# Half a fill tile set twice into the hand-made TensorE order of each of the first six attention steps

## The chip, the cores and the metric

The kernel runs on one core of a Trainium2 chip. The metric is the device time of one execution in microseconds (us). TensorE does the matmuls; VectorE, ScalarE and GpSimd do the element work; SyncE issues most of the transfers. In the rows they are called PE (its weight loads PEld), DVE, ACT, POOL and SP.

## The reference, cut to what matters

One layer on 1024 tokens of width 1024, float32. `x @ w_in` is split into three branches: an attention with three kinds of keys (compressed, selected, window), a gated MLP and an mLSTM. Their results are gated, merged, projected and normalised. The change concerns the attention and a few of the projections:

```python
(a_q, a_kc, a_vc, a_ks, a_vs, a_kw, a_vw, a_g, a_z,
 b_u, b_v, b_z,
 c_q, c_k, c_v, c_if, c_o, c_z, m_g) = jnp.split(x @ w_in[i], split_at, axis=-1)
y_a = _nsa(a_q, a_kc, ..., cmp_wv2[i]) * jax.nn.silu(a_z)
y_b = _spatial_gating(b_u, b_v, ..., sg_b[i]) * jax.nn.silu(b_z)
```

`_nsa` works on two groups of four heads. For each block of 128 queries it makes a softmax over 63 compressed keys; these weights also rank the 16 key blocks of which 8 are selected. A softmax over the selected keys and one over a window of 256 keys follow, and the three results are added with gates. `_spatial_gating` starts with `gelu(b_u)`.

## The kernel before

A float32 operand of a large product is held as the sum of two rounded halves (`hi`, `lo`), and three matmuls take the place of one. All large projections are made that way. A projection tile of 128 outputs by 1024 tokens is done in two halves of 512 tokens; a half is 8 x 3 = 24 matmuls into one bank of PSUM (`proj_half`, L127, PSUM tag `pj`, two banks).

Most of the program is put in order by a scheduler. In the attention (`attend`) the order of TensorE's instructions is written out by hand: inside `tc.manual_schedule` they go out as the code issues them. Instructions from outside that block may still be placed between them by the scheduler. The other engines are ordered by the scheduler. Each engine executes its own list.

`attend(g)` first makes keys and queries (`prep_group`: KA/KB, QA/QB; 144 matmuls of L127). Then follow nine steps. In step s:

- `attn_max(g, s)`: for each of four heads scores against the window keys (`ps_w`, L487) and the selected keys (`ps_s`, L495), and on VectorE the row maxima (`rowmax`, L408 and L411). At its end the maxima are transposed (`ps_m`, L502), and VectorE writes them into QB (L503).
- `Back(g, s-1)`: scores again, transposed and exponentiated (`ps_st`, L529 and L530, L532), values (`ps_o`, L557, with four updates of `o` on VectorE for each kind of key, L564 to L568), and in `finish` two transposes of the result (`ps_ot`, L574), copied to `ya` (L577).
- `attn_cmp`: compressed scores for query block s+1 (`ps_c`, L425), softmax on VectorE and ScalarE (`pcm`, L427 to L436), from block 4 on the ranking `rk` (L440 to L457). At the end of the step the weights are transposed (`ps_t`, L461), and from block 4 on the ranking is transposed too (`ps_r`, L466) and written into QB (L467). The product with the compressed values (`ps_co`, L471) comes in the next step.

`ps_c`, `ps_t`, `ps_r`, `ps_co`, `ps_w`, `ps_s` and `ps_m` share the PSUM tag `m`, which has two banks. So each of them also waits for the reader of the last but one.

Fill tiles are projections that the attention doesn't need: `fill_bu` (gelu), `fill_bz` and `fill_az` (silu), each 2 x 24 matmuls, with a ScalarE operation and one to three VectorE operations on each half (for `bu` L170 to L173; for `bz` L179, L180 and L607). Their weights are loaded, rounded on ScalarE (L90) and subtracted on VectorE (L91) in `load_w`. In the kernel before they are called after `attend`, outside the hand-made order: three `bu` and three `bz` behind group 0, the rest behind group 1.

Of the kernel before, what the change touches and what calls it, by code (L numbers as in the profile page):

```python
# [2 lines left out]

# [1 line left out]

# [18 lines left out]
KT = 8  # L24
# [19 lines left out]
def hybrid_kernel(ctx, tc, xm, pT, wfm, wvg, wtm, cmpw1, cmpw2, cpos, vecs, sgwT, sgb,  # L44
# [4 lines left out]
    stop = dbg.get("stop")  # L49
# [19 lines left out]
    def pj():  # L69
        return pst("pj", 2)  # L70

    mm = nc.tensor.matmul
# [48 lines left out]
    def proj_half(po, w, half, hs, ls, K=KT, M=P):  # L121
        wh, wl = w
        n = 3 * K
        i = 0
        for k in range(K):
            for a, b in ((wh, hs), (wl, hs), (wh, ls)):
                mm(po[:M, :], lhsT=a[:, k, :], rhs=b(k, half), start=(i == 0), stop=(i == n - 1))  # L127
                i += 1

    def proj_tok(po, ws, tt, n, hs, ls):  # L130
# [34 lines left out]
    def gelu2(dst, src, n):  # L165

        sq = tp.tile([P, 512], F32, tag="ge_a", bufs=2, name="ge_a")[:, :n]
        if len(src.shape) == 3:
            sq = sq.rearrange("p (a b) -> p a b", a=src.shape[1])
        act(sq, src, AF.Square, scale=GK)  # L170
        stt(out=sq, in0=sq, scalar=1.0, in1=src, op0=OP.add, op1=OP.mult)
        act(sq, sq, AF.Tanh, scale=GC)
        stt(out=dst, in0=sq, scalar=1.0, in1=src, op0=OP.add, op1=OP.mult)  # L173
# [79 lines left out]
    wh = pc.tile([P, 8, 288], F32R, name="wh")  # L253
    wl = pc.tile([P, 8, 288], F32R, name="wl")
# [3 lines left out]
    for m in range(4):  # L258
        for r, half in ((0, 0), (0, 1), (1, 0), (1, 1)) if m == 0 else ((0, 0), (1, 0), (0, 1), (1, 1)):
            k = 2 * m + r  # L260
            for kv, w in enumerate((wk, wv)):
                for i, (a, b) in enumerate(((w[0], xh), (w[1], xh), (w[0], xl))):
                    mm(pkv[kv][half], lhsT=a[:, k, :], rhs=b(k, half), start=(k == 0 and i == 0),
                       stop=(k == KT - 1 and i == 2))
# [16 lines left out]
    for kv in range(2):  # L281
        st = stk[kv]
        for half in range(2):
            po = pkv[kv][half]
            a = half * 512
# [17 lines left out]
    for tt in range(NT):  # L303
        po = pst("o", 2, "ps_v")
# [8 lines left out]
    for kv in range(2):  # L313
        st = stk[kv]
        ph = pst("m", 2)
        for v in range(2):
            zb = yp.tile([P, T], F32, tag="y", bufs=YB, name="zb")
            z4 = zb[:, 0:1008].rearrange("p (j g n) -> p j g n", j=8, g=2)
            for j in range(8):
                i = 16 * v + 2 * j  # L320
                nc.any.tensor_scalar(out=z4[:, j], in0=st[:, :, i:i + 993:16], scalar1=pos[:, kv, 8 * v + j:8 * v + j + 1],
                                     scalar2=None, op0=OP.add)
            for j in range(8):
                mm(ph[:, 0:126], lhsT=w1[kv][v][:, j, :], rhs=zb[:, j * 126:j * 126 + 126],
                   start=(v + j == 0), stop=(v + j == 8))
# [9 lines left out]
        else:  # L335
            pvc = pst("m", 2)
            for g in range(G):
                mm(pvc[0:63, g * 64:g * 64 + 64], lhsT=ge[:, g * 63:g * 63 + 63], rhs=w2[:, 1, :],
                   start=True, stop=True)
# [241 lines left out]
    def fill_az(i):  # L581
        w = wf(FM["az"] + i)
        for half in range(2):
            po = pj()
            proj_half(po, w, half, xh, xl)
            y = ya[i][:, half * 512:half * 512 + 512]
            z = tp.tile([P, 512], F32, tag="ge_a", bufs=2, name="zz")
            act(z, po, AF.Tanh, scale=0.5)
            stt(out=z, in0=z, scalar=1.0, in1=po, op0=OP.add, op1=OP.mult)
            stt(out=y, in0=z, scalar=0.5, in1=y, op0=OP.mult, op1=OP.mult)  # L590

    def fill_bu(i):
        w = wf(FM["bu"] + i)
        for half in range(2):
            po = pj()
            proj_half(po, w, half, xh, xl)
            gelu2(yb[i][:, half * 512:half * 512 + 512], po, 512)

    def fill_bz(i):
        w = wf(FM["bz"] + i)  # L600
        for half in range(2):
            po = pj()
            proj_half(po, w, half, xh, xl)
            z = tp.tile([P, 512], F32, tag="ge_a", bufs=2, name="zz")
            silu2(z, po, 512, z)
            y = yb[i][:, half * 512:half * 512 + 512]
            vv.tensor_mul(y, y, z)  # L607

    def attend(g):
        with tc.manual_schedule(engines={mybir.EngineType.PE}):
            d = prep_group(g)
            cmp_ = attn_cmp(g, 0, d)
            next(cmp_)
            next(cmp_)
            for step in range(NT + 1):
                back = Back(g, step - 1, d) if step else None
                mxs = attn_max(g, step, d) if step < NT else iter(())
                nmx = (4 + HPG * (1 + step // 4)) if step < NT else 0  # L620
                last = back.n if back else 2
                done = 0
                for k in range(last + 1):
                    upto = nmx * (k + 1) // (last + 1)
                    mid = (done + upto + 1) // 2
                    for _ in range(done, mid):
                        next(mxs)
                    if back and k < back.n:
                        back.scores(k)
                    for _ in range(mid, upto):  # L630
                        next(mxs)
                    done = upto
                    if k == 0:
                        if step < NT:
                            next(cmp_)
                        cmp_ = attn_cmp(g, step + 1, d) if step + 1 < NT else iter(())
                        next(cmp_, None)
                    if back and k:
                        back.values(k - 1)
                if back:  # L640
                    back.finish()
                next(mxs, None)
                next(cmp_, None)
    attend(0)
    for i in range(3):
        fill_bu(i)
        fill_bz(i)
    attend(1)
    fill_bu(3)
    fill_bz(3)  # L650
    for i in range(4):
        fill_az(i)
    if "ya" in dbg:
        for i in range(4):
            nc.sync.dma_start(dbg["ya"][i], ya[i])
# [387 lines left out]
    for b in range(3):  # L1043
# [7 lines left out]
        for n in range(8):  # L1051
            if n % 2 == 0:
                wb = load_w(wbr[b, n // 2], 8, P)
            w = (wb[0][:, 4 * (n % 2):4 * (n % 2) + 4, :], wb[1][:, 4 * (n % 2):4 * (n % 2) + 4, :])
# [19 lines left out]
    for n in range(8):  # L1074
        w = load_w(wout[n], KT, P)
# [3 lines left out]
        for half in range(2):  # L1079
            s = slice(half * 512, half * 512 + 512)  # L1080
            po = pj()
# [52 lines left out]
    for tt in range(NT):  # L1134
# [5 lines left out]
        for c in range(npc):  # L1140
            s = slice(c * n, c * n + n)
            pe = pst("m" if tt == 1 else "o", 2, "ps_e")
            i = 0
# [147 lines left out]
```

## Time and profile before

| | |
|---|---|
| device time, median of 3 runs | 1373.07 us (1372.04 to 1374.55) |
| profiled execution, its device time | 1371.17 us |
| span from its first to its last instruction | 1369.1 us |
| mean granted TensorE clock in it | 0.993 of full |
| TensorE busy | 1337.7 us, 98% of the span |
| VectorE busy | 844.4 us, 62% |
| ScalarE busy | 526.1 us, 38% |
| GpSimd busy | 152.8 us, 11% |

All rows come from one profiled execution. Times in rows count from the start of its span. A matmul's duration in a row includes its way through the array, and the next one starts before it ends; so the rate of a run of matmuls is read from the distance of their starts. A bracket at the end of a row gives the idle time of the engine ahead of the row and what ended it. The granted clock is 1.00 at 2.4 GHz and 0.50 at 1.2 GHz.

### The profile page before, as it was taken

How to read it: one execution, taken by the hardware profiler on the slowest of the kernel's cores; microseconds unless marked ns; L12 is line 12 of the kernel's file. 1: busy time of each engine (PE TensorE's matmuls, PEld its weight loads, DVE VectorE, ACT ScalarE, POOL GpSimd, SP SyncE). 2: the span in 40 equal slices, each digit the busy share in tenths (PEclk: the TensorE clock that was granted, in tenths of full speed). 3: DMA queues.
4: the chain of work that ended last, by engine and by line, in shares of the span. 5: the costliest groups of instructions: out<-in, count | busy, mean ns of one | idle time of the engine just before them, and what ended most of it. 6: DMA issues, size and time to landing. Idle time of an engine off the chain costs nothing.

```text
span 1369.1 us, 18928 instructions
## 1 busy us (share of the span) xinstructions
PE 1337.7 (98%) x7135; PEld 1130.5 (83%) x7135; DVE 844.4 (62%) x1991; ACT 526.1 (38%) x1059; POOL 152.8 (11%) x173
## 2 busy tenths in 40 slices
PE   8998999998999999999999999999999999999997
PEld 6986888886888899988888888888878887888786
DVE  6247777336777467647776678766544555334855
ACT  6354333344333343135455355553442212324211
POOL 0012211101120100001001000010000444000312
PEclk9999999999999999999999999999999999999999
DMA  9131001111002141333223332236346543114201
GB/s 316 32 71 50 24 28 28 38 48 43 9 24 69 41 155 54 132 108 124 82 73 108 108 110 79 81 120 212 108 169 208 194 152 108 47 62 126 105 32 47
DMA packets 48059, 127.46 MB, mean 93 GB/s; under 512 B 5208, under 2 KB 16344, under 8 KB 47968
## 3 DMA queue, kind: packets, MB, share of 16 engines
q1 hardware_dynamic: 47008, 123.11, 27.4%
q0 software_dynamic: 960, 3.15, 1.1%
q8 instruction: 56, 0.92, 0.3%
q14 instruction: 35, 0.29, 0.1%
HBM read 101.00 MB, written 25.23 MB: 92 GB/s over the span
## 4 chain that ended last, share of the span: by engine, by line
PE 90%; DVE 5%; ACT 2%; DMA 2%; issue 1%; SPq 0%; POOL 0%; DVEq 0%; ACTq 0%; POOLq 0%
PE ps_pj L127 19%; PE ps_a L837 14%; PE ps_b L127 9%; PE ps_b L837 8%; PE ps_o L557 7%; PE ps_g L1106 5%; PE ps_st L148 3%; PE ps_pj L148 3%; PE ps_c L837 3%; PE ps_st L529 2%; PE ps_st L530 2%; PE ps_v L136 2%; PE ps_e L1146 2%; PE ps_s L495 1%; PE ps_w L487 1%
## 5 line engine op out<-in xcount | busy, mean ns | idle before, releaser
L127 PE MATMUL ps_pj<-xh,whi 128*128 128x512 f32 x288 | 115.5, 401 | 2.3 <-DVE QA L401 2.3
L127 PE MATMUL ps_pj<-xh,wlo 128*128 128x512 f32 x288 | 115.2, 400 | 0.0
L127 PE MATMUL ps_pj<-xl,whi 128*128 128x512 f32 x288 | 114.6, 398 | 0.0
L557 PEld LDWEIGHTS ps_o<-V,pt 128*128 128x128 f32 x912 | 110.2, 191 | 3.4
L557 PE MATMUL ps_o<-V,pt 128*128 128x65 f32 x912 | 108.3, 271 | 0.0
L532 ACT ACTIVATE pt<-ps_st 128x512 f32<-128x512 f32 x114 | 62.8, 596 | 89.3 <-PE ps_st L530 88.6
L837 PE MATMUL ps_a<-op_lo,sh 128*128 128x512 f32 x240 | 94.1, 392 | 0.0
L837 PE MATMUL ps_a<-op_hi,sl 128*128 128x512 f32 x240 | 93.8, 391 | 0.0
L837 PE MATMUL ps_a<-op_hi,sh 128*128 128x512 f32 x240 | 93.8, 391 | 0.0
L824 DVE TENSOR_TENSOR sl<-ss,sh 128x512 fp32r<-128x512 f32 x80 | 54.8, 690 | 59.0 <-ACT sh L823 58.9
L90 ACT CAST whi<-wraw 128x1024 fp32r<-128x1024 f32 x46 | 48.3, 1049 | 94.8 <-PE ps_b L127 44.7
L127 PE MATMUL ps_b<-sp_hi,wlo 128*128 128x512 f32 x192 | 74.8, 390 | 1.3 <-DVE wlo L91 1.3
L127 PE MATMUL ps_b<-sp_lo,whi 128*128 128x512 f32 x192 | 74.7, 389 | 0.0
L91 DVE TENSOR_TENSOR wlo<-wraw,whi 128x1024 fp32r<-128x1024 f32 x46 | 62.3, 1353 | 19.7 <-ACT whi L90 15.5
L127 PE MATMUL ps_b<-sp_hi,whi 128*128 128x512 f32 x192 | 73.9, 389 | 0.0
L1065 POOL TENSOR_TENSOR M<-M,gt 128x512 f32<-128x512 f32 x32 | 43.8, 1378 | 199.1 <-DVE gt L1064 183.5
L127 PEld LDWEIGHTS ps_pj<-xh,whi 128*128 128x128 f32 x288 | 54.3, 188 | 13.7 <-PE ps_pj L127 3.9
L127 PEld LDWEIGHTS ps_pj<-xh,wlo 128*128 128x128 f32 x288 | 54.3, 188 | 10.0
L127 PEld LDWEIGHTS ps_pj<-xl,whi 128*128 128x128 f32 x288 | 54.3, 189 | 9.3
L823 ACT CAST sh<-mraw 128x512 fp32r<-128x512 f32 x60 | 37.4, 623 | 57.1 <-PE ps_a L837 30.8
L823 ACT CAST sh<-ss 128x512 fp32r<-128x512 f32 x80 | 49.6, 620 | 22.9 <-PE ps_b L837 22.1
L824 DVE TENSOR_TENSOR sl<-mraw,sh 128x512 fp32r<-128x512 f32 x60 | 43.6, 727 | 22.8 <-ACT sh L823 22.8
(369 smaller groups left out, 3534.2 us busy)
## 6 DMA issues: line engine op xcount, KB each, us to landing
mraw<-in_wfm_dram SPq DMA_DIRECT2D x40, 512.0 KB, 3.6
gsc<-gt SPq DMA_DIRECT2D x24, 512.0 KB, 2.6
gt<-gsc SPq DMA_DIRECT2D x24, 512.0 KB, 4.3
wraw<-in_wfm_dram SPq DMA_DIRECT2D x18, 512.0 KB, 3.5
xraw<-in_xm_dram SPq DMA_DIRECT2D x14, 512.0 KB, 5.5
yraw<-ysc SPq DMA_DIRECT2D x12, 512.0 KB, 3.4
wraw<-in_wbr_dram SPq DMA_DIRECT2D x12, 512.0 KB, 5.0
wraw<-in_wtm_dram SPq DMA_DIRECT2D x8, 512.0 KB, 4.0
```

Source lines behind the costliest of these rows:

```text
L90: nc.scalar.copy(hi[:, c], raw[:, c])
L91: vv.tensor_sub(lo[:, c], raw[:, c], hi[:, c])
L127: mm(po[:M, :], lhsT=a[:, k, :], rhs=b(k, half), start=(i == 0), stop=(i == n - 1))
L136: mm(po[:, :n], lhsT=tok(a, k, tt), rhs=b[:, k % 4, :], start=(i == 0), stop=(i == tot - 1))
L148: mm(po, lhsT=tok(a, 4 * i + k, tt), rhs=b[:, k, :], start=(i == 0 and tt % 2 == 0 and k == 0 and j == 0), stop=(i == 1 and k == 3 and j = ...
L532: act(pt.rearrange("p h q -> p (h q)"), sp, AF.Exp)
L557: mm(po[:, h * 65:h * 65 + 65], lhsT=pt[:, h, :], rhs=V[:, j, vi, :], start=(first and h == 0), stop=last, skip_group_check=True)
L823: nc.scalar.copy(hi, src)
L824: vv.tensor_sub(lo, src, hi)
L837: mm(bank, lhsT=l[a][:, k, :], rhs=r[b], start=first and k == 0 and i == 0, stop=k == K - 1 and i == 2, skip_group_check=True)
L1065: nc.gpsimd.tensor_add(M[n][:, s], M[n][:, s], t[:, s])
L1106: mm(po[:, 0:n], lhsT=a[k][:, ts_], rhs=b[k][:, s], start=(k == 0 and i == 0), stop=(k == KT - 1 and i == 2))
```

## The change

`fill_*` become generators. `proj_parts` does what `proj_half` did, and yields once in the middle; the fill functions pass that on and yield again behind each half with its epilogue. One `next(fills)` is therefore half a half tile: 12 matmuls. `attend` takes a generator and calls `next(fills)` twice in each of steps 0 to 5, inside the hand-made order: once behind the first row-maximum matmul of the step (ahead of the first scores), and once ahead of `back.finish()`. Twelve calls use up `bu(0)`, `bz(0)`, `bu(1)` in group 0 and `bu(3)`, `bz(3)`, `az(0)` in group 1. The other six fill tiles stay outside, called after `attend`, as all were.

```diff
+    def proj_parts(po, w, half, hs, ls):
+
+        wh, wl = w
+        i = 0
+        for k in range(KT):
+            if k == KT // 2:
+                yield
+            for a, b in ((wh, hs), (wl, hs), (wh, ls)):
+                mm(po, lhsT=a[:, k, :], rhs=b(k, half), start=(i == 0), stop=(i == 3 * KT - 1))
                 i += 1
...
     def fill_bu(i):
         w = wf(FM["bu"] + i)
         for half in range(2):
             po = pj()
-            proj_half(po, w, half, xh, xl)
+            yield from proj_parts(po, w, half, xh, xl)
             gelu2(yb[i][:, half * 512:half * 512 + 512], po, 512)
+            yield
...
-    def attend(g):
+    def attend(g, fills):
...
                     for _ in range(done, mid):
                         next(mxs)
+                    if k == 0 and step < 6:
+                        next(fills)
                     if back and k < back.n:
                         back.scores(k)
...
                     if back and k:
                         back.values(k - 1)
+                if step < 6:
+                    next(fills)
                 if back:
                     back.finish()
                 next(mxs, None)
                 next(cmp_, None)
-    attend(0)
-    for i in range(3):
-        fill_bu(i)
-        fill_bz(i)
-    attend(1)
-    fill_bu(3)
-    fill_bz(3)
-    for i in range(4):
-        fill_az(i)
+    fl = chain(fill_bu(0), fill_bz(0), fill_bu(1))
+    attend(0, fl)
+    for _ in chain(fl, fill_bz(1), fill_bu(2), fill_bz(2)):
+        pass
+    fl = chain(fill_bu(3), fill_bz(3), fill_az(0))
+    attend(1, fl)
+    for _ in chain(fl, fill_az(1), fill_az(2), fill_az(3)):
+        pass
```

How the lists of the engines move is shown at two places. The fills carry the line L127 before and L139 after; the other lines move down by 12 or a little more (L425 becomes L437, L461 L473, L487 L499, L502 L514, L503 L515, L568 L580, L574 L586). The text keeps the numbers of before. A line of "..." stands for more rows of the same run of fills.

TensorE at the head of group 0, from the compressed scores of query block 0 (`ps_c`) on. Before:

```order
L425 MATMUL ps_c<-kbd_201,q_968 128x128 x2
L127 MATMUL ps_pj<-xh,whi 128x512
L127 MATMUL ps_pj<-xh,wlo 128x512
...
L461 MATMUL ps_t<-ident,pcm 128x128 x2
L487 MATMUL ps_w<-KBw,QB 128x128
L127 MATMUL ps_pj<-xh,wlo 128x512
L127 MATMUL ps_pj<-xl,whi 128x512
L487 MATMUL ps_w<-KBw,QB 128x128
L471 MATMUL ps_co<-vbd_203,pts 128x128 x2
```

And after:

```order
L437 MATMUL ps_c<-kbd_201,q_968 128x128 x2
L473 MATMUL ps_t<-ident,pcm 128x128 x2
L499 MATMUL ps_w<-KBw,QB 128x128
L139 MATMUL ps_pj<-xh,whi 128x512
L139 MATMUL ps_pj<-xh,wlo 128x512
...
L499 MATMUL ps_w<-KBw,QB 128x128
L483 MATMUL ps_co<-vbd_203,pts 128x128 x2
```

Before, 28 fills stand between `ps_c` and the transpose `ps_t` of its softmax, and two between the first two `ps_w`. Now none stands ahead of `ps_t`, and twelve stand between the first two `ps_w`. On VectorE and ScalarE the order is the same in both up to the last operation of that softmax (L436).

TensorE at the end of step 3, from the last values (`ps_o`) to the first `ps_w` of step 4. Before, with 20 fills between the values and the first of these rows:

```order
L574 MATMUL ps_ot<-ident,o 128x128
L127 MATMUL ps_pj<-xh,wlo 128x512
L127 MATMUL ps_pj<-xl,whi 128x512
L574 MATMUL ps_ot<-ident,o 128x128
L502 MATMUL ps_m<-ident,mx 8x128
L461 MATMUL ps_t<-ident,pcm 128x128 x2
L127 MATMUL ps_pj<-xh,whi 128x512
...
L466 MATMUL ps_r<-ident,rk 16x128
L127 MATMUL ps_pj<-xh,whi 128x512
...
L487 MATMUL ps_w<-KBw,QB 128x384
```

And after, with the block of twelve fills shown by its last row:

```order
L139 MATMUL ps_pj<-xl,whi 128x512
L586 MATMUL ps_ot<-ident,o 128x128 x2
L514 MATMUL ps_m<-ident,mx 8x128
L473 MATMUL ps_t<-ident,pcm 128x128 x2
L478 MATMUL ps_r<-ident,rk 16x128
L499 MATMUL ps_w<-KBw,QB 128x384
L139 MATMUL ps_pj<-xh,whi 128x512
```

The three fills between `ps_t` and `ps_r` and the six between `ps_r` and `ps_w` are gone, and the next fills come behind the first `ps_w`.

VectorE at the same place. Before, from the last scaling factors to the ranking's cast:

```order
L566 TENSOR_TENSOR osc<-osc,gates 128x4
L457 TENSOR_SCALAR rk<-rk 128x16
L568 SCALAR_TENSOR_TENSOR o<-ps_o,osc,o 128x64 x4
L577 COPY ya<-ps_ot 128x128
L503 TENSOR_TENSOR QB<-ps_m,nblk 8x512
L180 SCALAR_TENSOR_TENSOR zz<-zz,ps_pj 128x512
L467 CAST QB<-ps_r 16x512
L607 TENSOR_TENSOR yb<-yb,zz 128x512
```

And after:

```order
L192 SCALAR_TENSOR_TENSOR zz<-zz,ps_pj 128x512
L469 TENSOR_SCALAR rk<-rk 128x16
L578 TENSOR_TENSOR osc<-osc,gates 128x4
L621 TENSOR_TENSOR yb<-yb,zz 128x512
L580 SCALAR_TENSOR_TENSOR o<-ps_o,osc,o 128x64 x4
L451 MEMSET im 128x1
L92 TENSOR_TENSOR wlo<-wraw,whi 128x1024
L515 TENSOR_TENSOR QB<-ps_m,nblk 8x512
L479 CAST QB<-ps_r 16x512
```

The two operations on the fill's half tile (`zz` from `ps_pj`, and `yb`) now stand ahead of the four updates of `o`, and the weight conversion `wlo` stands ahead of the write of the maxima into QB. Before, the updates of `o` came first, and the two fill operations were set around the ranking's cast.

## Rows read from the trace of the kernel before

**Rows 1.** The page, engine table: busy us, share, instructions of TensorE and its loads first.

```profile
PE 1337.7 (98%) x7135; PEld 1130.5 (83%) x7135; DVE 844.4 (62%) x1991; ACT 526.1 (38%) x1059; POOL 152.8 (11%) x173
```

**Rows 2.** TensorE's waits: instruction, released by: us in total, times, longest.

```profile
PE ps_ot L574 <- DVE o L568: 6.5, 2, 3.3
PE ps_pj L127 <- DVE QA L401: 2.3, 4, 0.7
```

**Rows 3.** Timeline of TensorE, group 0, end of step 1: start, duration, instruction.

```profile
123.71 0.77 PE L574 MATMUL ps_ot<-ident,o 128*128 128x128 f32 x2 [3.25 <-DVE o L568]
124.28 0.42 PE L502 MATMUL ps_m<-ident,mx 128*8 128x128 f32 x1
...
125.47 0.69 PE L487 MATMUL ps_w<-KBw,QB 128*128 128x384 f32 x1 [0.35 <-DVE QB L503]
125.95 0.63 PE L529 MATMUL ps_st<-QA,KAw 128*128 128x512 f32 x1
...
127.66 0.39 PE L487 MATMUL ps_w<-KBw,QB 128*128 128x384 f32 x1
```

**Rows 4.** Timeline of VectorE, the same place.

```profile
120.03 0.08 DVE L411 DVE_READ_ACCUMULATOR2_ANT mx<- 128x1 f32 x1
...
121.96 1.22 DVE L91 TENSOR_TENSOR wlo<-wraw,whi 128x1024 fp32r<-128x1024 f32 x1
123.10 0.85 DVE L568 SCALAR_TENSOR_TENSOR o<-ps_o,osc,o 128x64 f32<-128x64 f32 x4
124.73 0.68 DVE L503 TENSOR_TENSOR QB<-ps_m,nblk 8x512 fp32r<-8x512 f32 x1 [0.78 <-PE ps_m L502]
```

**Rows 5.** Stretch 120 to 130: busy us by engine, granted clock, DMA share, GB/s.

```profile
120.00:130.00 10.00, 6.40 (x30) 4.73 (x28) 7.64 (x29) 2.57 (x6) 1.06 (x2) 0.66 0.19 52
```

**Rows 6.** Timeline of TensorE, head of group 0.

```profile
98.25 0.60 PE L425 MATMUL ps_c<-kbd,q 128*128 128x128 f32 x4
98.61 0.48 PE L127 MATMUL ps_pj<-xh,whi 128*128 128x512 f32 x1
...
103.93 0.39 PE L127 MATMUL ps_pj<-xl,whi 128*128 128x512 f32 x1
...
106.04 0.41 PE L461 MATMUL ps_t<-ident,pcm 128*128 128x128 f32 x2
```

**Rows 7.** Timeline of VectorE, head of group 0: the softmax's first and last operation.

```profile
98.90 0.42 DVE L427 TENSOR_TENSOR pcm<-ps_c,cb 128x256 f32<-128x256 f32 x1 [1.77 <-PE ps_c L425]
...
105.47 0.43 DVE L436 TENSOR_TENSOR pcm<-pcm,sm 128x256 f32<-128x256 f32 x1
```

**Rows 8.** Matmuls of L127 by stretch: us, TensorE busy with them (count), clock, DMA.

```profile
98.50:113.30 14.80, 11.95 (x44) 1.00 0.19 53
113.60:125.40 11.80, 1.33 (x4) 0.81 0.14 33
125.60:140.50 14.90, 6.37 (x23) 0.93 0.15 40
140.70:159.90 19.20, 8.87 (x34) 1.00 0.03 8
160.20:180.80 20.60, 8.54 (x33) 1.00 0.16 45
```

**Rows 9.** Timeline of TensorE, end of step 3.

```profile
157.30 0.27 PE L502 MATMUL ps_m<-ident,mx 128*8 128x128 f32 x1
...
159.99 0.44 PE L487 MATMUL ps_w<-KBw,QB 128*128 128x384 f32 x1
```

**Rows 10.** Timeline of VectorE, end of step 3.

```profile
159.97 0.69 DVE L607 TENSOR_TENSOR yb<-yb,zz 128x512 f32<-128x512 f32 x1
```

**Rows 11.** Timeline of ScalarE, end of step 3.

```profile
157.39 0.60 ACT L179 ACTIVATE zz<-ps_pj 128x512 f32<-128x512 f32 x1 [8.75 <-PE ps_pj L127]
```

**Rows 12.** Timeline of TensorE, late in step 4.

```profile
172.28 0.59 PE L495 MATMUL ps_s<-KBs,QB 128*128 128x128 f32 x2
```

**Rows 13.** Timeline of VectorE, late in step 4.

```profile
174.33 0.28 DVE L411 CUSTOM_DVE_ANT_0 junk<-ps_s,cr 128x128 bf16<-128x128 f32 x1
```

More of the change, by code (lines that the diff above doesn't have):

```diff
@@ L2 @@
 from contextlib import ExitStack
+from itertools import chain
 import numpy as np
@@ L127, in proj_half @@
                 mm(po[:M, :], lhsT=a[:, k, :], rhs=b(k, half), start=(i == 0), stop=(i == n - 1))
+                i += 1
+    def proj_parts(po, w, half, hs, ls):
[6 more added lines that the diff above has]
+                mm(po, lhsT=a[:, k, :], rhs=b(k, half), start=(i == 0), stop=(i == 3 * KT - 1))
                 i += 1
@@ L595, in fill_bu @@
             po = pj()
-            proj_half(po, w, half, xh, xl)
+            yield from proj_parts(po, w, half, xh, xl)
             gelu2(yb[i][:, half * 512:half * 512 + 512], po, 512)
+            yield
     def fill_bz(i):
@@ L602, in fill_bz @@
             po = pj()
-            proj_half(po, w, half, xh, xl)
+            yield from proj_parts(po, w, half, xh, xl)
             z = tp.tile([P, 512], F32, tag="ge_a", bufs=2, name="zz")
@@ L607, in fill_bz @@
             vv.tensor_mul(y, y, z)
-    def attend(g):
+            yield
+    def attend(g, fills):
         with tc.manual_schedule(engines={mybir.EngineType.PE}):
```

## The prediction

> **What bounds the kernel now.** I read the engine table first: TensorE is busy for 98% of the span [rows 1]. So only two things can move the time: idle time of TensorE, and the rate at which it works. The list of TensorE's waits comes next. Within the attention its largest entry is the pair of output transposes, `ps_ot`, which wait for VectorE's `o`: 6.5 us in two waits, one in each group [rows 2]. The timeline of TensorE puts that wait at the end of step 1 [rows 3]: the transposes start at 123.71, after 3.25 us of idling. VectorE shows why [rows 4]: the last update of `o` ends at 123.95 by its row, because a conversion of fill weights (L91, 1.22 us) stands ahead of it. After the wait four matmuls of 512 columns, from 125.95 to 127.66, go at 0.43 us each, where the fills of the head go at (103.93 - 98.61)/23 = 0.23 us [rows 3, 6]. The stretch from 120 to 130 has a mean granted clock of 0.66 [rows 5]: 6.8 us of it at 1.2 GHz, the rest at 2.4.
>
> Last I read what the fills cover. From the first `ps_c` of group 0 to the first `ps_w` of step 1 there are 44 of them, then 4, 23, 34 and 33 in the stretches up to the first `ps_w` of steps 2, 3, 4 and 5 [rows 8]. In steps 3 and 4 TensorE hardly idles at all, so the single fills between the hand-set instructions sit where those instructions have to wait.
>
> **The head of a group.** `ps_c` goes out at 98.25, and `ps_t` transposes its softmax at 106.04 [rows 6]. The softmax starts on VectorE at 98.90 and its last product ends at 105.47 + 0.43 = 105.90 [rows 7]. In between the two engines do the rest of the QA and QB work, a weight conversion and the exponentials. Before, TensorE runs 28 fills there. After the change `ps_t` stands right behind `ps_c`, while VectorE and ScalarE have the same order up to that product. From about 98.85, when `ps_c` is through, to 106.04 TensorE idles: **7.2 us**. Nothing hides it; this is the surest term.
>
> **The middles of the steps.** The pairs of `ps_m` banks make `ps_w` and `ps_s` wait for VectorE's maxima. By the order of before 9, 4, 7, 3 and 15 fills stand in these places in steps 0 to 4; at 0.23 us that is at most 2.1, 0.9, 1.6, 0.7 and 3.4 us of new idling, and at least 0, if VectorE turns out to be early. The nearest rows are those of step 4: two `ps_s` are out at 172.28 + 0.59 = 172.87, and VectorE takes the maximum that frees the bank for the next from 174.33 to 174.62 [rows 12, 13]. That is 1.75 us of waiting under ten fills worth 2.3 us, so most of the cover is needed. I take **2.1, 0.9, 1.4, 0.4 and 2.2**.
>
> **The ends of the steps.** Here the block of 12 fills (12 x 0.23 = 2.8 us) ahead of `ps_ot` hides the update of `o`. At the end of step 1 it replaces the idle 3.25 us, and VectorE no longer has the weight conversion there: **-3.25 us**. But behind `ps_ot` come `ps_m`, `ps_t`, from step 3 on `ps_r`, and the next `ps_w`, with no fill between them any more. `ps_w` needs VectorE's L503 (0.68 us [rows 4]) on `ps_m`, and from step 3 on L467 of the same size on `ps_r`. Before, `ps_m` to `ps_w` took 159.99 - 157.30 = 2.7 us at the end of step 3 with 9 fills inside [rows 9]. What else stands in VectorE's queue is new. The block completes its tile just there, so the tile's own ScalarE operation (0.60 us [rows 11]) and VectorE operation (0.69 us, as the product in [rows 10]) follow it at once, in VectorE's order ahead of L503 at the ends of steps 1 and 2.
> - Step 0: L503 alone, less what TensorE does meanwhile: **1.0** us (0.7 to 1.4).
> - Steps 1 and 2: 0.2 + 0.60 + 0.69 + 0.68 = 2.2 us after the block, less 0.75 us of transposes: **1.4** each (0.7 to 2.2).
> - Step 3: VectorE has the block's first operation, two small ones (0.3), the block's second operation (0.69) and only then the four updates of `o` (0.85 [rows 4]). So `ps_ot` waits 0.2 + 0.60 + 0.69 + 0.3 + 0.69 + 0.85 = 3.3 us. Then come L91 (1.22), L503 and, after `ps_r` (0.3), L467: `ps_w` goes out 6.2 us after the block. Less 0.8 us of transposes: **5.4** (3.0 to 6.2).
> - Step 4: the copy of `ya` (0.3), L503, another fill operation, L467: 3.0 us, less 0.8: **2.2** (1.4 to 3.0).
> - Step 5: the same 3.0 us with 9 fills inside: **0.4** (0 to 0.9).
>
> **The sum for a group.** New idling: 7.2 + (2.1 + 0.9 + 1.4 + 0.4 + 2.2) + (1.0 + 1.4 + 1.4 + 5.4 + 2.2 + 0.4) = 26.0 us. Old waits that go: 3.25, the 0.35 ahead of `ps_w` [rows 3], and about 0.6 for QA (2.3/4 [rows 2]): 4.2 us. Up to step 6 the fills stand in 17 runs and no longer in 36. The first fill behind a small float32 matmul has 0.48 us instead of 0.39 [rows 6], so 19 x 0.09 = 1.7 us are saved. The first two blocks hold two thirds of the head's former fills only; the rest is done later at the same rate and costs nothing of its own.
>
> **The clock.** The dip that goes with the 3.25 us wait is a cost of before. Of its 6.8 us the last slow matmuls, up to about 127.7 [rows 3], mark the end, so it began near 120.9, and 2.8 us of it passed before TensorE resumed at 123.71. The other 4.0 us cost at most half of that, 2.0 us; a part of them were waits, and I put it at 1.6 us. After the change the head (7.2 us idle) and the end of step 3 (3.3 us, then almost 2.5 more with little work) are longer than the wait that was followed by a dip, so I count two dips in each group. Dense fills follow both, so about 4 us of work at half rate cost 2.0 us each. The clock's part is 2 x 2.0 - 1.6 = +2.4 us. It could be one dip (+0.4), or five, one for every thinly used stretch (+8.4).
>
> The Trainium skill (TensorE: Matmul & The Clock Gate, Terms) prices throttled time at that time times the share of the clock lost, half of it here. For the 6.8 us measured this would be 3.4 us a dip and +3.4 us a group in place of +2.4, hence 2 us more in the total. The rows stand against it, because a clock that is low while TensorE idles takes nothing, and that was the case for 2.8 of the 6.8 us. My sum uses the rows.
>
> A group loses 26.0 - 4.2 - 1.7 + 2.4 = 22.5 us. Group 1 is ordered in the same way on TensorE and VectorE (its 3.25 us wait is the second in [rows 2]), so the total is +45 us. The profiled execution took 1371.17 us, which gives 1416; the median of the runs is 1.9 us higher, hence **1418 us**. With every low end and one dip a group loses 13.7 - 4.2 - 1.7 + 0.4 = 8.2 us (1389 us); with every high end and five dips 31.8 - 4.2 - 0.9 + 8.4 = 35.1 (1443).
>
> **Rivals.**
> - *Thin stretches keep the clock low* (five dips): 2 x 3 x 2.0 = 12 us more, 1430. For it: in the 54 us that steps 0 to 2 then take TensorE idles for 15.4. Against it: waits of half a microsecond each, such as those for QA, show no dip.
> - *VectorE runs ahead*: with fewer epilogues crowded together, half of the 18.8 us that I put behind the head is not waited for: 2 x 9.4 less, 1399. For it: in the middles of the steps every price is a bound from covered waits. Against it: the orders at the ends of the steps are fixed.
> - *Waiting instructions are passed* (the other side): if TensorE ran the fills while an instruction ahead of them waits, the 26.0 us would vanish, and with them the new dips; the 4.2, the old dip and the 1.7 us would remain as gain: 2 x 7.5 = 15 us, 1358. It decides from the point at which more than four fifths of the new idling is filled in this way. The Trainium skill (TensorE: Matmul & The Clock Gate, the table at its head) gives the engine a partial reorder window. It names only weight loads as what is pulled ahead. The rows say no: the last maximum for `ps_m` was done by 120.11 [rows 4], yet `ps_m` stayed behind the waiting `ps_ot` until 124.28 [rows 3].
> - *Nothing moves*: the same matmuls are done, TensorE is 98% busy, and each new wait takes the place of an old one: 1373. Against it: inside the attention only some 4 us a group are there to be replaced.
>
> **How the numbers follow.** Forecast (1405 to 1428) 0.50; five dips 0.17; VectorE ahead 0.22; passing 0.06; nothing moves 0.04; further off 0.01. The first three and the rest end slower by more than 0.2% (which is about what a measurement of this kernel can tell from no change): 0.90; same 0.04; faster 0.06. The range 1394 to 1436 takes in the forecast and nearly all of the first two rivals.
>
> **What would show it.** In the profile of the changed kernel TensorE's busy share falls to about 95%. The list of its waits is led by `ps_t` waiting for `pcm`, about 7 us in each group, and `ps_ot` still waits for `o`, but at the end of step 3 and not of step 1. `ps_w` waits for `QB` at every end of a step. The granted clock shows 0.5 after the head and after step 3. I am wrong if `ps_t` goes out within 2 us of `ps_c`, if fills execute while `ps_t` waits, or if the time from the head's `ps_c` to the first `ps_w` of step 4 (159.99 - 98.25 = 61.7 us before [rows 6, 9]; I expect 15 more) grows by less than 6 us.

## The result, and the profile after

The changed kernel takes 1423.3 us (median of 4 runs, 1420.4 to 1426.9) against 1373.0 us of the kernel before: a ratio of 1.037, with a 95% interval of 1.034 to 1.039. The forecast was 1418 us with a range of 1394 to 1436, slower. The profiled execution took 1423.16 us, its span 1421.4 us, 52.3 us longer than before. Line numbers are now higher by 12 to 14 (`ps_t` stands in L473, the mask row in L515, the update of `o` in L580), and the fills have a line of their own, L139.

The engine table of the changed kernel, TensorE's row and the granted clock in 40 slices:

```profile
PE 1355.9 (95%) x7135; PEld 1145.6 (81%) x7135; DVE 844.7 (59%) x1993; ACT 525.1 (37%) x1057; POOL 152.3 (11%) x173
...
PEclk9999989998999999999999999999999999999998
```

TensorE has as many matmuls and 95% instead of 98% [rows 1]. The list of its waits (total us, times, longest) shows with what it idles:

```profile
PE ps_t L473 <- DVE pcm L448: 14.3, 2, 7.1
PE ps_s L507 <- DVE mx L423: 6.1, 10, 1.8
PE ps_ot L586 <- DVE o L580: 5.3, 2, 2.6
PE ps_w L499 <- DVE QB L479: 4.9, 4, 1.5
PE ps_w L499 <- DVE QB L515: 3.2, 2, 1.6
PE ps_w L499 <- ACT pts L475: 3.0, 4, 0.9
PE ps_r L478 <- ACT pts L475: 2.1, 4, 0.6
```

Most of this is new: in the whole list of before `ps_ot` had 6.5 us [rows 2], at another place, `ps_s` 1.3 us behind the maxima and `ps_w` 0.7 us behind `QB`, and the other rows have no counterpart in it. The order of the list is what a reader should look at: the head of the group is first, the maxima in the middles of the steps second, and the other five rows are ends of steps. TensorE's timeline shows the head and the end of step 3 of group 0 (start, duration, instruction, and in brackets the idle time and what ended it):

```profile
98.17 0.60 PE L437 MATMUL ps_c<-kbd,q 128*128 128x128 f32 x4
105.91 0.66 PE L473 MATMUL ps_t<-ident,pcm 128*128 128x128 f32 x2 [7.13 <-DVE pcm L448]
...
169.58 0.62 PE L586 MATMUL ps_ot<-ident,o 128*128 128x128 f32 x2 [2.64 <-DVE o L580]
...
171.12 0.38 PE L478 MATMUL ps_r<-ident,rk 128*16 128x128 f32 x1 [0.60 <-ACT pts L475]
172.44 0.69 PE L499 MATMUL ps_w<-KBw,QB 128*128 128x384 f32 x1 [0.94 <-DVE QB L479]
172.93 0.63 PE L139 MATMUL ps_pj<-xh,whi 128*128 128x512 f32 x1
```

Between `ps_c` and `ps_t` nothing runs; that stretch held 28 fills before [rows 6]. The block of step 3 ended at 166.55 + 0.39, then `ps_ot` waited. VectorE's timeline shows for what:

```profile
167.60 0.69 DVE L192 SCALAR_TENSOR_TENSOR zz<-zz,ps_pj 128x512 f32<-128x512 f32 x1 [1.09 <-ACT zz L191]
...
168.36 0.69 DVE L621 TENSOR_TENSOR yb<-yb,zz 128x512 f32<-128x512 f32 x1
168.96 0.85 DVE L580 SCALAR_TENSOR_TENSOR o<-ps_o,osc,o 128x64 f32<-128x64 f32 x4
169.74 1.22 DVE L92 TENSOR_TENSOR wlo<-wraw,whi 128x1024 fp32r<-128x1024 f32 x1
...
170.99 0.68 DVE L515 TENSOR_TENSOR QB<-ps_m,nblk 8x512 fp32r<-8x512 f32 x1
171.71 0.68 DVE L479 CAST QB<-ps_r 16x512 fp32r<-16x512 f32 x1
```

The two operations that finish the block's tile go ahead of the four updates of `o`, and a weight conversion goes ahead of the two writes to `QB` that `ps_w` needs.

The windows of group 1, cut at the first `ps_w` of each step (head, then steps 0 to 5; the first number behind PE is its busy time, PEclk the mean granted clock):

```profile
338.60:346.80 8.20, 1.07 (x9) 0.86 (x7) 4.39 (x11) 5.40 (x17) 1.44 (x2) 0.69 0.27 80
346.80:360.00 13.20, 11.55 (x46) 8.84 (x44) 5.34 (x25) 2.67 (x11) 1.44 (x2) 0.81 0.04 11
360.00:374.70 14.70, 12.18 (x65) 9.76 (x65) 9.91 (x42) 5.24 (x15) 2.66 (x4) 1.00 0.03 9
374.70:391.50 16.80, 14.80 (x86) 12.44 (x86) 11.02 (x42) 5.30 (x18) 2.72 (x4) 1.00 0.14 40
391.50:413.80 22.30, 17.84 (x106) 15.03 (x106) 16.79 (x55) 7.08 (x19) 3.98 (x6) 0.99 0.06 10
413.80:440.20 26.40, 22.56 (x121) 18.95 (x121) 15.42 (x58) 6.42 (x18) 3.99 (x6) 0.88 0.06 23
440.20:467.20 27.00, 26.96 (x153) 22.91 (x153) 16.28 (x58) 7.75 (x20) 4.20 (x6) 0.94 0.02 5
```

The clock is low in four of the seven windows. A mean of 0.69 between levels of 0.5 and 1 means that 2 x 0.31 x 8.2 = 5.1 us of the window ran at 1.2 GHz. Summed in this way over all seven windows group 1 has 20.1 us at half clock. In group 0 the low matmuls stand behind the same four places (head, end of step 3, middle and end of step 4).

The loss lies almost wholly in the attention: the last `ps_ot` of group 1 starts 49.7 us later than before (530.17 against 480.44), of the 52.3 us between the spans.

### The profile page after: what moved, and what is told of

It reads as the page before. It is cut to its first block, busy times and chain, and to the rows that moved or that the text cites. A ratio compares the mean times of both kernels' runs of the same rounds, so it can differ in the third digit from the quotient of the medians.

```text
span 1421.4 us, 18929 instructions
## 1 busy us (share of the span) xinstructions
PE 1355.9 (95%) x7135; PEld 1145.6 (81%) x7135; DVE 844.7 (59%) x1993; ACT 525.1 (37%) x1057; POOL 152.3 (11%) x173
## 3 DMA queue, kind: packets, MB, share of 16 engines
q1 hardware_dynamic: 47008, 123.11, 26.3%
## 4 chain that ended last, share of the span: by engine, by line
PE 85%; DVE 7%; ACT 3%; DMA 3%; issue 2%; SPq 0%; POOL 0%; DVEq 0%; ACTq 0%; POOLq 0%
PE ps_a L855 13%; PE ps_pj L128 10%; PE ps_pj L139 10%; PE ps_b L128 9%; PE ps_b L855 7%; PE ps_o L569 7%; PE ps_g L1124 5%; PE ps_c L855 3%; PE ps_st L160 2%; PE ps_pj L160 2%; PE ps_st L541 2%; PE ps_st L542 2%; PE ps_v L148 2%; PE ps_e L1164 1%; PE ps_s L507 1%
## 5 line engine op out<-in xcount | busy, mean ns | idle before, releaser
L139 PE MATMUL ps_pj<-xh,whi 128*128 128x512 f32 x192 | 83.3, 434 | 0.0
L139 PE MATMUL ps_pj<-xh,wlo 128*128 128x512 f32 x192 | 82.1, 428 | 0.0
L139 PE MATMUL ps_pj<-xl,whi 128*128 128x512 f32 x192 | 80.7, 420 | 0.0
L423 DVE CUSTOM_DVE_ANT_0 junk<-ps_w,cr 128x384 bf16<-128x384 f32 (+2 forms) x64 | 32.3, 504 | 45.8 <-PE ps_w L499 44.5
L1124 PE MATMUL ps_g<-gh,sp_lo 128*128 128x512 f32 (+1 forms) x144 | 52.7, 366 | 0.0
L1124 PE MATMUL ps_g<-gh,sp_hi 128*128 128x512 f32 (+1 forms) x144 | 52.7, 366 | 0.0
```

Source lines behind the costliest of these rows:

```text
L139: mm(po, lhsT=a[:, k, :], rhs=b(k, half), start=(i == 0), stop=(i == 3 * KT - 1))
L1124: mm(po[:, 0:n], lhsT=a[k][:, ts_], rhs=b[k][:, s], start=(k == 0 and i == 0), stop=(k == KT - 1 and i == 2))
```

## The experiments

All are timed beside the kernel before on the same chip; its median was 1371.7 us in the first four and 1372.8 us in the others. Where two of them are compared, each is first taken against its own median.

**The head covered.** The two blocks of step 0 go into the head.

```diff
             next(cmp_)
+            next(fills)
+            next(fills)
             next(cmp_)
...
-                    if k == 0 and step < 6:
+                    if k == 0 and 0 < step < 6:
...
-                if step < 6:
+                if 0 < step < 6:
```

> The changed kernel, with the two blocks of step 0 moved into the head of the group: 24 fills now stand between ps_c and the first ps_t, and none in step 0. The theory that the loss is idle time in fixed places: the wait of ps_t falls from 7.13 us to 7.13 - 24 x 0.23 = 1.6 us, the half clock behind the head goes (it cost 1.5 us in group 0, 2.3 us in group 1), and step 0, without fills, lasts about as long as its chain of row maxima on VectorE, 6 to 7 us in place of 12.3 us from the first ps_t to the first ps_w of step 1. So 5 to 7 us less in each group, 1423 - 12 = about 1411 us. The rival, that the fills merely run out and any place left bare costs the same: step 0 gets all that the head gives back, 1420 to 1424 us.

Measured: 1420.5 us, ratio 1.035 (1.033 to 1.037), which is the number of the rival in the expectation. Its reason is not quite the rival's, though. The wait of `ps_t` fell as worked out, from 7.13 to 1.73 us in group 0 and 1.72 us in group 1. Step 0 gave part of that back (0.40, 0.41 and 1.53 us of waits), so the idle time up to step 6 fell from 21.5 to 17.7 us in group 0. The clock took the rest. The windows of the head and steps 0 to 2, group 0:

```profile
98.00:106.40 8.40, 6.67 (x34) 5.33 (x32) 4.80 (x12) 6.02 (x18) 1.47 (x2) 1.00 0.27 78
106.40:114.80 8.40, 5.42 (x21) 4.10 (x20) 6.02 (x26) 2.34 (x10) 1.44 (x2) 0.53 0.05 16
114.80:134.10 19.30, 16.52 (x68) 12.89 (x66) 8.94 (x40) 5.00 (x15) 2.67 (x4) 0.76 0.03 8
134.10:150.90 16.80, 14.81 (x86) 12.43 (x86) 11.00 (x42) 5.26 (x18) 3.28 (x5) 1.00 0.20 56
```

The head and steps 0 and 1 of the changed kernel, group 0:

```profile
98.00:106.20 8.20, 1.07 (x8) 0.87 (x7) 4.39 (x11) 5.40 (x17) 1.44 (x2) 0.79 0.29 80
106.20:118.50 12.30, 10.70 (x45) 8.23 (x43) 5.25 (x25) 2.67 (x11) 1.44 (x2) 0.86 0.04 11
118.50:133.30 14.80, 12.23 (x66) 9.81 (x66) 10.01 (x42) 5.24 (x15) 2.66 (x4) 1.00 0.04 11
```

The head has the full clock now, but step 0, bare of fills, has 0.53 and step 1 has 0.76 and lasts 19.3 us; in the changed kernel it lasts 14.8 us at 1.00. So the same fills can be put elsewhere and the half clock goes with the bare place. In group 1 this is weaker: step 0 has 0.60, step 1 has 0.90 and lasts 16.2 us.

**Idle work in the head.** Extra matmuls whose result is overwritten.

```diff
+            if half == 0 and i in (0, 3):
+                for r in range(30):
+                    mm(po, lhsT=w[0][:, r % 8, :], rhs=xh(r % 8, half), start=(r == 0), stop=(r == 29))
+                yield
             yield from proj_parts(po, w, half, xh, xl)
...
             next(cmp_)
+            next(fills)
             next(cmp_)
```

> The changed kernel, with 30 extra matmuls of 128x512 between ps_c and the first ps_t of each group, 30 x 0.23 = 6.9 us of work whose result is overwritten. They fit into the 7.13 us in which TensorE waits, so the waiting itself stays a loss. If the half clock behind the head comes of the idling, it goes, and the time falls by what that half clock cost: 1.5 us in group 0 and 2.3 us in group 1 by the fills at 0.43 us, a little more with the other matmuls there: 1418 to 1420 us. If it would come anyway, or costs nothing, 1423 us. If the extra matmuls push ps_t out, over 1424 us.

Measured: 1422.5 us (1.035 to 1.039), no difference from the changed kernel that can be told. The extra work fitted in: `ps_t` started at 105.94 after 0.37 us of idling. What the clock did differs between the groups. The windows of the head, step 0 and step 1 of group 0, and of the same three of group 1 (its first also holds the end of the preparation):

```profile
98.10:106.10 8.00, 7.63 (x37) 6.10 (x37) 4.42 (x11) 5.42 (x17) 1.47 (x2) 1.00 0.26 82
106.10:118.30 12.20, 10.66 (x45) 8.20 (x45) 5.30 (x25) 2.67 (x11) 1.45 (x2) 0.86 0.04 12
118.30:136.20 17.90, 15.43 (x65) 12.62 (x65) 9.95 (x41) 5.19 (x15) 2.67 (x4) 0.81 0.03 8
339.90:349.60 9.70, 9.33 (x45) 7.52 (x44) 4.85 (x12) 5.61 (x18) 1.73 (x3) 1.00 0.22 68
349.60:360.40 10.80, 9.18 (x45) 7.06 (x44) 5.26 (x25) 2.67 (x11) 1.44 (x2) 1.00 0.04 12
360.40:375.20 14.80, 12.25 (x66) 9.83 (x66) 10.01 (x42) 5.26 (x15) 2.67 (x4) 1.00 0.04 11
```

The head's half clock is gone in both. In group 0 two others came, in steps 0 and 1, behind waits of 0.2 to 0.6 us. The changed kernel has the same waits at the same places, and the fills behind them go at the full rate (0.23 us). In group 1, with the same order and nearly the same waits, none came in these steps. So step 1 took 17.9 us in one group and 14.8 us in the other. My reading that a dip belongs to one long wait was too simple.

**Tiles that end at the start of a step.** One block moves from the end of step 5 to step 0, so that no tile is finished ahead of `ps_ot`.

```diff
                     if k == 0 and step < 6:
                         next(fills)
+                        if step == 0:
+                            next(fills)
...
-                if step < 6:
+                if step < 5:
                     next(fills)
```

> The changed kernel, with one block of 12 fills moved from the end of step 5 to the first place of step 0 (24 fills stand there). So every later tile is completed by the block at the start of a step and not by the one ahead of ps_ot, and the operations of VectorE that finish a tile no longer stand ahead of the updates of o and of the mask row of QB at the ends of steps 1 to 3. The theory that these operations make the ends of the steps long: the wait of ps_ot at the end of step 3 falls from 2.64 us to below 1 us, those of ps_w for QB at the ends of steps 1 and 4 (1.58 and 1.46 us) each by about 0.7 us, and one half clock goes: 3 to 6 us in each group, 1411 to 1417 us. The rival, that VectorE has the same work and the wait only moves to the row maxima in the middle of the steps: within 3 us of 1423 us. The wait of ps_t in the head stays at 7.1 us by both.

Measured: 1418.3 us (1.032 to 1.035), 5 us less than the changed kernel and just short of what the theory asked. The end of step 3 of group 0:

```profile
177.96 0.62 PE L586 MATMUL ps_ot<-ident,o 128*128 128x128 f32 x2 [0.78 <-DVE o L580]
...
179.51 0.28 PE L478 MATMUL ps_r<-ident,rk 128*16 128x128 f32 x1 [0.60 <-ACT pts L475]
180.56 0.44 PE L499 MATMUL ps_w<-KBw,QB 128*128 128x384 f32 x1 [0.77 <-DVE QB L479]
```

`ps_ot` waits 0.78 us and no longer 2.64: the operations that finish the tile were what stood ahead of `o`. But the rival was half right too. New waits came in the middles of the steps (in both groups 0.93 us for the maxima and 0.52 us for `o` in step 0 and 0.65 us for `o` in step 3, in group 1 also 0.68 us in step 4), and the idle time up to step 6 fell by 4.5 us in group 0 and 3.0 us in group 1 only. The clock stayed as in the changed kernel, 0.982 on average.

**One tile by hand.** Only the first fill tile of each group is set by hand, its two halves of 24 matmuls (the "pair of tiles" of the expectations), in units of 3; the change sets three tiles by hand. `adv(n)` calls `next(fills)` n times. The scheduler keeps the rest.

```diff
-            if k == KT // 2:
+            if k:
                 yield
...
             next(cmp_)
+            adv(10)
             next(cmp_)
...
-                    if k == 0 and step < 6:
-                        next(fills)
+                    if k == 0 and step < 2:
+                        adv((1, 1)[step])
...
-                if step < 6:
-                    next(fills)
+                if step < 2:
+                    adv((0, 4)[step])
...
-    fl = chain(fill_bu(0), fill_bz(0), fill_bu(1))
-    attend(0, fl)
+    attend(0, fill_bu(0))
```

> Only one pair of fill tiles of each group is set by hand: 30 matmuls in the head, 3 in each of the middles of steps 0 and 1, 12 at the end of step 1 ahead of ps_ot. All other fills are left to the scheduler, which places those of the next tile one by one from step 0 on. If the loss of the change comes of taking from the scheduler the fills that covered the other waits, and not of setting fills by hand, this kernel has neither the loss nor the waits of 3.25 us for o and the half clock behind them that the kernel before has: 1373 - 2 x (3.25 + 0.35 + 0.8 to 1.6) = 1362 to 1365 us. If hand-set fills cost by themselves, over 1380 us. If the scheduler's fills only make up for one another, 1371 to 1375 us.

Measured: 1362.8 us, ratio 0.994 (0.992 to 0.995): faster than the kernel before by 0.6%, little but outside the interval. In the list of waits nothing for `pcm`, `o` or `QB` is left among the first ten rows. Its first two, and the one of the scheduler's fills, which wait half a microsecond in each group for `yb`, the operation that finishes the first hand-set half:

```profile
PE ps_w L499 <- ACT pts L475: 2.1, 2, 1.1
PE ps_pj L275 <- ACT xh L212: 1.7, 1, 1.7
...
PE ps_pj L139 <- DVE yb L185: 1.0, 2, 0.5
```

The windows of the head and steps 0 to 2 of group 0 have the full clock:

```profile
98.00:106.30 8.30, 7.80 (x38) 6.21 (x37) 4.89 (x12) 6.02 (x18) 1.46 (x2) 1.00 0.26 79
106.30:114.50 8.20, 7.51 (x41) 5.27 (x39) 6.46 (x27) 2.34 (x10) 1.46 (x2) 1.00 0.05 16
114.50:126.70 12.20, 11.16 (x66) 9.33 (x65) 8.28 (x39) 4.17 (x16) 2.70 (x4) 1.00 0.04 13
126.70:142.60 15.90, 15.87 (x93) 13.46 (x93) 12.96 (x44) 7.05 (x20) 3.27 (x5) 1.00 0.19 59
```

So it is not the setting by hand that costs. Step 1 takes as long as before (12.2 us) and holds 24 fills instead of 4 [rows 8]: 12 of them are the block ahead of `ps_ot`, where 3.25 us were waited [rows 3], 3 are the unit in its middle, and the other 9 are fills of the next tile that the scheduler put between the hand-set instructions.

**The parts apart.** Two kernels: the change in steps 0 and 1 alone, and its complement, the placement of the kernel above in head and steps 0 and 1 with the blocks of the change in steps 2 to 5.

```diff
-                    if k == 0 and step < 6:
+                    if k == 0 and step < 2:
...
-                if step < 6:
+                if step < 2:
```

> Half of the change's idea kept: the blocks of steps 0 and 1 alone are set by hand, four of twelve in each group; the rest is left to the scheduler, which has a free tile from the middle of step 1 on. Counted with 0.23 us for each fill, head and steps 0 and 1 cost 7.9 us more in the changed kernel than before (35.1 us with 48 fills, against 27.2 us with 48), and steps 2 to 5 cost 18.6 us more. If the parts add up, this kernel loses 7 to 8 us in each group, 1373 + 15 = 1386 to 1389 us, with the wait of 7.13 us for pcm still first in the list. If the loss goes by the number of blocks, the same third of 50 us: 1389 us; so this run alone does not tell these two apart, its complement does. If most of the loss is the free tile that the scheduler is missing, it is below 1385 us.

Measured: 1378.7 us, ratio 1.005 (1.003 to 1.006). The head's wait is there in full:

```profile
PE ps_t L473 <- DVE pcm L448: 14.3, 2, 7.2
PE ps_h L1038 <- DVE nb L1036: 1.5, 4, 0.4
```

The kernel is only 6.0 us longer than the one before, but these 6 us are a difference. New are the 14.3 us and 3.1 us of shorter waits in steps 0 and 1; gone are the old waits, 9.8 us in both groups together, as the scheduler's free fills came back from the middle of step 1 on. That makes 7.6 us, and the span is 7.4 us longer (1376.5 against 1369.1) with TensorE busy for 1337.7 us in both. What the bare head costs, with the short waits and the half clock that go with it, shows against the kernel with one tile by hand: that one sets the same 48 matmuls of a group by hand and differs only in where they stand. It is 8.9 us shorter than the kernel before, so the difference is 6.0 + 8.9 = 14.9 us. For the complement, which sets the three tiles of the change, the edit against the kernel with one tile by hand is:

```diff
-                    if k == 0 and step < 2:
-                        adv((1, 1)[step])
+                    if k == 0 and step < 6:
+                        adv((1, 1, 4, 4, 4, 4)[step])
...
-                if step < 2:
-                    adv((0, 4)[step])
+                if step < 6:
+                    adv((0, 4, 4, 4, 4, 4)[step])
```

> The complement: head and steps 0 and 1 by hand as in the kernel with one pair of tiles set by hand (30, 3, 3 and 12 matmuls), and in steps 2 to 5 the blocks of the change. No fill is left to the scheduler before step 5. By the sum of the stretches steps 2 to 5 cost 18.6 us in each group, and steps 0 and 1, without the free fills of a second tile, about as much as before: 1373 + 2 x 18.6 = 1410 us, 1402 to 1414 us. If the cost goes by the number of blocks, two thirds of 50 us: 1406 us, with the loss spread evenly. If the head is what starts all later trouble, as the half clock might suggest, 1375 to 1385 us.

Measured: 1411.3 us, ratio 1.028 (1.026 to 1.029). In the order of TensorE no free fill stands before step 5. Against the kernel with one tile by hand, which has the same matmuls in the same hand-set places up to step 1, the blocks of steps 2 to 5 cost 38.5 + 8.9 = 47.4 us. Not all of it passes in these steps: the scheduler's fills are missing in steps 0 and 1 too, and from the first `ps_c` of a group to the first `ps_w` of step 2 it takes 3.6 us longer in group 0 and 2.8 us in group 1. Measured from that kernel the whole change costs 50.3 + 8.9 = 59.2 us and its two parts 14.9 + 47.4 = 62.3 us, so they are near to additive. So it is not the head, the longest single wait, that carries most of the loss: about three quarters come with the blocks of steps 2 to 5, each of which takes fills away from the places where they covered something.

**Idle work in all long waits.**

```diff
+            next(fills)
+            idle(30)
...
+                if step == 3:
+                    idle(11)
                 if back:
                     back.finish()
                 next(mxs, None)
                 next(cmp_, None)
+                if 0 < step < 5:
+                    idle((0, 6, 3, 4, 6)[step])
```

Here `idle(n)` issues n matmuls of 128x512 into the bank of the next tile, which is opened one place earlier for it.

> The changed kernel with work that is overwritten put into its long waits: 30 matmuls of 128x512 in the head, 11 ahead of ps_ot in step 3, and 6, 3, 4 and 6 behind ps_t and ps_r at the ends of steps 1 to 4. They fit into the waits, so that the waits stay a loss and only the clock can change. If the half clock comes of thin stretches and these are now filled, the four dips of each group go, which cost 7.4 and 6.5 us by the fills at 0.43 us and some 2 us more in each group by other matmuls: 1405 to 1411 us. If they come back at other places, as one did in step 0 when the head alone was filled, 1414 to 1424 us. If the extra work does not fit, over 1424 us.

Measured: 1413.8 us (1410.1 to 1416.2), ratio 1.030 (1.028 to 1.031): 9.5 us less than the changed kernel, although 120 matmuls are added. It fell between the two lower ranges. In the profiled execution the four dips are gone, but group 0 has two at new places, in steps 0 and 1. That execution was the shortest of the four; its mean clock was 0.995, that of the others 0.990 to 0.993. The windows of group 1, cut as those of the changed kernel above:

```profile
333.10:341.20 8.10, 7.73 (x38) 6.19 (x37) 4.42 (x11) 5.43 (x17) 1.47 (x2) 1.00 0.26 81
341.20:352.00 10.80, 9.18 (x45) 7.07 (x44) 5.26 (x25) 2.68 (x11) 1.44 (x2) 1.00 0.05 12
352.00:366.80 14.80, 13.64 (x72) 10.87 (x72) 10.03 (x42) 5.30 (x15) 2.67 (x4) 1.00 0.04 11
366.80:383.50 16.70, 15.43 (x88) 12.82 (x88) 10.91 (x42) 5.28 (x18) 2.72 (x4) 1.00 0.13 40
383.50:405.90 22.40, 21.32 (x121) 17.74 (x121) 16.83 (x55) 7.11 (x19) 4.00 (x6) 1.00 0.06 12
405.90:429.30 23.40, 21.03 (x128) 17.96 (x128) 15.43 (x58) 6.43 (x18) 4.01 (x6) 1.00 0.07 25
429.30:454.70 25.40, 25.36 (x154) 21.82 (x153) 16.34 (x58) 7.77 (x20) 4.20 (x6) 1.00 0.02 6
```

This pair of tables measures the clock nearly alone. Where the changed kernel had the full clock (steps 1 to 3) the lengths agree within 0.1 us, so the extra work takes nothing; steps 0, 4 and 5 are shorter by 2.4, 3.0 and 1.6 us. The whole stretch takes 454.7 - 333.1 = 121.6 us against 467.2 - 338.6 = 128.6: **7.0 us** are the price of 20.1 us at half clock. Group 0 has half clock in steps 0 and 1 (means of 0.86 and 0.90, where the changed kernel has 0.86 and 1.00), and saved 5.7 us. The profiled execution, with 1410.1 us, was 13.0 us under that of the changed kernel, of which these two groups make up 12.7.

The Trainium skill (TensorE: Matmul & The Clock Gate, Terms) prices throttled time at the share of the clock lost, here 10 us for 20.1. The trace does not agree: 7.0 us. Part of the low time fell on waits: 5.1 of the 20.1 us lie in the head's window, where TensorE was busy for 1.07 of 8.2 us.

**One unit behind `ps_t`.** The kernel with one tile by hand, with three of its matmuls moved from the middle of step 1 behind `ps_t` at its end.

```diff
-                        adv((1, 1)[step])
+                        adv((1, 0)[step])
...
                 next(cmp_, None)
+                if step == 1:
+                    adv(1)
```

> The kernel with one pair of tiles set by hand, with three of its matmuls moved from the middle of step 1 to the place behind ps_t at the end of step 1, where ps_w waits 1.06 us. Three matmuls are 0.69 us: 0.7 us less in each group, 1361 to 1362 us, if the three that leave the middle of the step are made up for by the scheduler's own; 1362 to 1364 us if they are not.

Measured: 1361.9 us, ratio 0.992 (0.990 to 0.993). It has the lowest median of all, 11 us under the kernel before and 61 us under the change. The wait of 1.06 us is no longer in the trace. Whether it beats the kernel without this move is unclear: the intervals overlap.

## Right or wrong, step by step

The direction, the reason and the size held: new idling of TensorE, as no fill passes a waiting instruction, and 1423 us in the range of 1394 to 1436. The near agreement of the sum, 45 us forecast and 50 measured, hides terms that were off in opposite directions, new idling too high and the clock too low, so its closeness is in part luck.

- *Head*, 7.2 us: measured 7.13 in both groups. Right.
- *Middles of steps 0 to 4*, 2.1, 0.9, 1.4, 0.4 and 2.2 us: the waits are 0.9, 1.0, 1.1, 0.2 and 2.0 us, of which 0.4 each in steps 0 and 1 are old. 4.4 us new instead of 7.0. The bounds from fills by 0.23 us were too high above all in step 0.
- *Ends of steps 0 to 5*, 1.0, 1.4, 1.4, 5.4, 2.2 and 0.4 us: measured 0.6, 1.6, 0.9, 4.2 (2.64 + 0.60 + 0.94), 1.9 and 0. That step 3 is the worst, and the order on VectorE that makes it so, was right and is shown by the run whose tiles end earlier. Two of these waits I put down to the wrong engine: at the ends of steps 0 and 2 `ps_w` waits for ScalarE's copy of `pts`, as does `ps_r` in steps 3 and 4. The 0.2 us that the sums put between a block and the operations that finish its tile come from no row; at the end of step 3 ScalarE starts at 166.97, 0.03 us behind the block.
- *Old waits gone*, 4.2 us: 3.25, 0.35 and 0.51 us, right. New idling less old: 21.5 - 4.9 = 16.6 us in a group instead of 21.8.
- *Clock*, +2.4 us, two dips in a group: this is the term that was mis-sized. There are four places in each group, 20.1 us at half clock in group 1, and they cost 7.0 us there by the run with idle work. For the old one no run gives the price apart; its four slow matmuls [rows 3] make 0.8 us, and its 6.8 us at the rate of 7.0 to 20.1 would make 2.4 us (an estimate). So the term was 4.6 to 6.2 us. I had counted a dip only behind waits at least as long as the 3.25 us of before; the middle and end of step 4, with waits of 1.8, 0.5 and 1.5 us, got one each. The rival with five dips came nearer in this. The argument against it, that waits of half a microsecond show no dip, held in steps 1 and 2 of the changed kernel and failed in group 0 of the run with idle work in the head. Its 15.4 us of idling in "steps 0 to 2" include the head's 7.2.
- *Fragments*, -1.7 us (0.9 in the high end of the range, for which no reason is given): not to be found. The stretch to the first `ps_w` of step 6 is 23.8 us longer in group 0 with 11 fills fewer (166 against 177), which at 0.23 us makes 26.3. Idling (16.6) and the fills at 0.43 us (7.4 - 0.8 = 6.6) give 23.2. About 3 us stay unexplained; hand-set matmuls at half clock are in there, which I can't price one by one.
- *What would show it*: TensorE at 95%, yes; `ps_t` first with 7.1 us a group, yes; `ps_ot` waiting at the end of step 3 and not of step 1, yes; the time from the head's `ps_c` to the first `ps_w` of step 4 grew from 61.7 to 74.3 us, 12.5 instead of 15. `ps_w` waits for `QB` at the ends of steps 1, 3 and 4 only.

What the prediction did not see is the trade behind the sum. It priced the waits that the blocks leave bare, place by place, but took the fills as lost to the scheduler without asking how many had to be taken. One tile by hand in the head and ahead of `ps_ot`, with the next tile left free, removes the old waits and costs nothing; the same tile in the four blocks of steps 0 and 1 leaves the head bare and costs 14.9 us more; three tiles leave the scheduler nothing before step 5. What holds its fills back until then stays open: no run here varies the PSUM banks or the weight buffers of the fills.

## What to carry to other kernels

Where an engine's order is written by hand and filler work is left to a scheduler, hand-set filler covers the places you see and uncovers those that the scheduler was serving one matmul at a time, so set only what closes a known wait and leave the next tile to the scheduler. Count the work behind a block too: what finishes its tile lands in another engine's queue, and here it stood ahead of what the next instruction needed. Don't judge a change by the longest wait in the list, nor by its time against the kernel before alone: the 14.3 us at the head of the list made a kernel only 6.0 us longer, because old waits of 9.8 us went with the same edit, while many waits of at most 2.6 us, most of them in the later steps, with the clock that follows them, cost three times as much as the head.

## What was not expected of the hardware

- The same order with nearly the same waits had different clocks in the two groups. With idle work in the head, group 0 had half clock in steps 0 and 1 and group 1 had none there; in the complement of steps 2 to 5, group 0 had four stretches of fills at 0.43 us and group 1 two. The Trainium skill (TensorE: Matmul & The Clock Gate, What's actually happening) calls the number of slow matmuls run-variable for one kernel. The runs agree: the four executions of the kernel with all long waits filled had mean clocks of 0.990 to 0.995. The two groups show the like within a single execution, of which the page says nothing.
- Filling 14 us of waiting in each group with useless matmuls made a kernel 9.5 us faster, by the clock alone.
- A bare stretch moved its half clock along: with the fills of step 0 put into the head, group 0 had 1.00 in the head instead of 0.79, but 0.53 instead of 0.86 in step 0 and 0.76 instead of 1.00 in step 1.
